# Mixer of a hybrid decoder layer: all projections as pairs of chunks with sum quads, banks swapped by halves, two heads a stage, lent ring blocks at another byte

## The chip, the cores and the metric

The kernel runs on one core of one Trainium2 chip. The metric is the device time of one execution in microseconds (us), the median of three runs. The engines are named as in the profile: PE is TensorE (matmuls; PEld loads its weights), DVE is VectorE, ACT is ScalarE, POOL is GpSimd, SP is SyncE, which issues the weight transfers.

## The reference

One layer on 256 tokens of 2048 numbers, everything in fp32: two SwiGLU blocks with the mixer between them.

```python
x = x + 0.5 * swiglu(rmsnorm(x), ffn1_w_in, ffn1_w_out)      # 2048 -> 2*5632 -> 2048
h = rmsnorm(x) @ mix_w_in                                    # 2048 -> 13312 columns
b, c, xin, p, q, k, v, gates = split(h)                      # seven of 1024, three gates of 2048
yA = (b * conv3(c * xin)) @ conv_w_out                       # causal, 3 taps
yB = (scale * group_linear(trailing_mean(p) - p)) @ pool_w_out   # windows 2, 4, 8, 16
yC = attention(q, k, v) @ attn_w_out                         # 8 heads of 128, causal, ALiBi
x = x + (sig(gA) * yA + sig(gB) * yB + sig(gC) * yC) @ mix_w_out
x = x + 0.5 * swiglu(rmsnorm(x), ffn2_w_in, ffn2_w_out)
out = rmsnorm(x)
```

## The kernel before

**Steps.** Weights stream from HBM in steps of four 128x512 blocks (`raw`, 1 MB). ACT rounds a step to its high part (`whi`, line 287), DVE subtracts that from `raw` for the low part (`wlo`, line 291), and PE does each product as three matmuls: high times high, high times low, low times high. A step is of one of three kinds. A chunk step ("C") adds into a chunk, 512 output columns for 256 tokens. A pair step ("P") adds into two chunks at once, four blocks for a quad of 256 inputs; both take 24 matmuls of 128x512. A sum step ("S", a "sum quad") computes the same quad by Strassen's and Winograd's seven products instead of eight: 21 matmuls, but DVE first builds sums of the blocks in place (lines 296 to 299, four additions of 128x512), seven blocks have to be split instead of four, and the activations of that quad need sums of their own (`sum_forms`, `sums_of_parts`). A pattern such as "SPSPSPPP" names the eight quads of a pair.

**Banks.** PSUM has eight banks of 128x512, named K1, K6, K2, K4, K7, K5, K3, K22 (0 to 7). The results of a pair end in K2 and K4 (chunk a) and K3 and K22 (chunk b). The sum products end in K1, K6, K7 and K5; DVE and ACT take them out early, behind the last S, in three pieces: `e1` (lines 529 and 530: K1, K6), `e2` (533: K7, K5) and `e3` (536: K5). At the end of the pair `results` adds them to chunk a and chunk b (542, 543).

**Side runs.** Between the halves of a step PE does small work of the mixer in the free banks (`side_psum`): eight transposes, scores of a head, products with V, the group linear. Each such function waits in a list and runs one at a time, `DELAY` and `GAP` half steps apart; its DVE and ACT work is queued right behind it, in program order.

**The mixer.** Before, the projections are 14 chunks of 4 C steps, in the order q, k (twice), v, v, then c, x, b (twice), p, p; then come gates A, B and C, each as two pairs ("SPSPSPPP", the first of A "PPPPPPPP") with two chunks of the branch's output projection behind each pair; then the output projection as four chunks. FFN1 stands ahead of the mixer and FFN2 behind it; both are pairs with sum quads already.

**Ring and units.** The split weights lie in a ring of 20 blocks. Ten of them stay; a region R of 8 and a region T of 2 are lent to the mixer as buffers ("units") between the end of FFN1 and, for R, the start of the gates, for T the start of FFN2. T's two blocks begin at bytes 185184 and 189280 of a partition; in the two FFNs 480 matmuls read them, in runs of 12.

**The first pair.** Its results are copied from their banks to `ev` (ACT line 562, DVE line 561) before the SwiGLU reads them, since the second pair wants the same banks.

Of the kernel before, what the change touches and what calls it, by code (L numbers as in the profile page):

```python
# [9 lines left out]
F32 = mybir.dt.float32  # L10
# [19 lines left out]
GATES = {(b, j): PATTERNS[0 if (b, j) == ("A", 0) else 3] for b in "ABC" for j in (0, 2)}  # L30
# [4 lines left out]
LEND = 10  # L35
REGIONS = {"R": (10, 18, "right"), "T": (18, 20, "left")}
# [35 lines left out]
def hybrid_trunk(ctx: ExitStack, tc: tile.TileContext, x, xT, wst, vecs, poolw, fnorm, consts, out):  # L72
# [118 lines left out]
    def side_psum():  # L191

        at = steps[cur[0]]
        assert side_open()
        if at["kind"] != "C":
            return wide(take(K1, K7))
        return wide(take(4, 6) if at["far"] else 6)

    def side_bank():

        at = steps[cur[0]]
        b = take(6, 7) if at["kind"] == "C" else take(K1, K6)
        return bank[:, b].rearrange("p (k s) -> p k s", s=S)
# [8 lines left out]
    def chunk(lhs, nk, evac, at=(0, 2), far=True, tail=False):  # L212


        ch = {}
        for i in range(nk):
            steps.append(dict(kind="C", lhs=lhs, i=i, first=i == 0, last=i == nk - 1, evac=evac, tail=tail,
                              chunk=ch, at=at, far=far, items=("W",)))

    def pair(forms, pattern, early, evac):  # L220
# [3 lines left out]
        mine = []  # L224
        for q, kind in enumerate(pattern):
# [13 lines left out]
            mine.append(dict(kind=kind, q=q, forms=forms, set=st, mm=mm, last=q == len(pattern) - 1, evac=evac,  # L239
# [121 lines left out]
    def emit_pair(n, half):  # L361
# [39 lines left out]
    deferred = deque()  # L401
# [76 lines left out]
    def x_side(n, j, st):  # L478
        def go():
# [47 lines left out]

    def e1():
        nc.scalar.activation(ev[:, 0], bank[:, K1], AF.Copy)
        nc.vector.tensor_sub(ev[:, 3], ev[:, 0], bank[:, K6])  # L530

    def e2():
        nc.vector.tensor_add(ev[:, 1:3], bank[:, K7:K7 + 2], ev[:, 3:4].to_broadcast((P, 2, CH)))

    def e3():
        nc.vector.tensor_add(ev[:, 3], ev[:, 1], bank[:, K5])

    def results(pattern):

        a, b = bank[:, K2:K2 + 2], bank[:, K3:K3 + 2]  # L540
# [6 lines left out]
    def in_set(n, xs, c, gs, pattern):  # L547
# [10 lines left out]
        def evac():  # L558
            a, b = results(pattern)
            if c + n == 0:  # L560
                nc.vector.tensor_copy(ev[:, 0:2], a)
                nc.scalar.activation(ev[:, 2:4], b, AF.Copy)  # L562
                a, b = ev[:, 0:2], ev[:, 2:4]
            nxt = steps[cur[0] + 1]["kind"]
            if "S" in pattern and nxt != "C":
                deferred.append((now[0] + 4, functools.partial(gate, a, b)))
# [28 lines left out]
    def ffn(n, xs, after):  # L595
# [3 lines left out]
        for p, cnt in enumerate(PARTS):  # L599
# [3 lines left out]
            for j in range(4):  # L603
# [10 lines left out]
                chunk(lambda i, c0=c0: gs[c0 + i], cnt, None if last else ev_o, at=((4, 0, 4, 2)[j],), far=False,  # L614
# [13 lines left out]
    def after1(j):  # L628
# [14 lines left out]
    xm = plain_of(x1)  # L643
# [14 lines left out]
    def ev_qk(c):  # L658
        base = keep_scaled("k", "r")

        def ev(acc):
            base(acc)
            q_, k_ = tok["q"], tok["k"]
            hold = {}

            def tr(hh):
                def go():
                    ps = side_psum()
                    for t in range(NT):
                        nc.tensor.transpose(ps[:, 0, t * P:(t + 1) * P], q_[:, t, hh * P:(hh + 1) * P], idn)  # L670
                        nc.tensor.transpose(ps[:, 1, t * P:(t + 1) * P], k_[:, t, hh * P:(hh + 1) * P], idn)
                    if hh % 2 == 0:
                        hold["qk"] = unit("qkT", F32)
                    v = hold["qk"][:, 2 * (hh % 2):2 * (hh % 2) + 2]
                    nc.scalar.activation(v, ps[:, 0:2], AF.Copy)
                    qkT[4 * c + hh] = v
                    if hh == 3:
                        drop(q_, k_)
                    if hh % 2:
                        qk_unit[4 * c + hh] = hold["qk"]  # L680
                return go
            later(*[tr(hh) for hh in range(4)])
        return ev

    def ev_v(c):
        base = keep_scaled("v")

# [10 lines left out]
    def attention(h):  # L698
# [509 lines left out]
```

## Time and profile before

| | us |
|---|---|
| median of 3 runs (lowest, highest) | 2272.11 (2270.14, 2273.11) |
| the profiled execution, its span | 2272.37, 2270.6 |
| PE, DVE, ACT busy in the span | 2250.7, 1608.9, 1084.7 |
| FFN1, projections, gates, output projection, FFN2 | 708, 368, 392, 90, 713 |

The span is what the profiler saw of the execution; 1.8 us lie around it. The stages of the last row are cut by eye at round times, where the lines of the matmuls change.

### The profile page before, as it was taken

The page shows a single profiled execution, that of the slowest core. Times are in us where ns is not written, and L with a number is a line of the kernel's source. Part 1 is how long each engine was busy: PE and PEld are TensorE (multiplying, and loading weights), DVE is VectorE, ACT ScalarE, POOL GpSimd, SP SyncE. Part 2 cuts the span into 40 slices and gives each one's busy share as a digit, 9 for nine tenths or more (in the row PEclk, how much of TensorE's full clock was granted, in tenths as well). Part 3 has the DMA queues.
Part 4 walks back from the last instruction along what each step waited for, and adds up shares of the span by engine and source line. Part 5 has one row for each costly group of instructions (what it writes and reads, how often), then busy time and mean ns, then how long its engine had stood idle before and what let it go on. Part 6 is the DMA issues. An engine that isn't in the chain of part 4 may idle for free.

```text
span 2270.6 us, 24723 instructions
## 1 busy us (share of the span) xinstructions
PE 2250.7 (99%) x10121; PEld 1857.9 (82%) x10121; DVE 1608.9 (71%) x1485; ACT 1084.7 (48%) x1040; POOL 3.7 (0%) x9
## 2 busy tenths in 40 slices
PE   9999999999999999999999999999999999999998
PEld 7888888888888888888888887888888888888887
DVE  6876885877875445555777887555876885887874
ACT  6544453454454445444555554454444453454452
POOL 0000000000000000000000000000000000000000
PEclk9999999999999999999999999999999999999999
DMA  9464564464463654455455555544564554464462
GB/s 338 167 227 147 219 222 166 173 236 167 185 241 132 220 189 182 165 203 180 185 196 212 222 201 186 209 183 178 187 230 149 221 223 149 185 241 167 186 241 93
DMA packets 65425, 442.83 MB, mean 195 GB/s; under 512 B 7328, under 2 KB 8096, under 8 KB 13472
## 3 DMA queue, kind: packets, MB, share of 16 engines
q1 hardware_dynamic: 65312, 441.26, 52.8%
q8 instruction: 79, 1.29, 0.2%
q14 instruction: 34, 0.28, 0.0%
HBM read 437.04 MB, written 4.19 MB: 194 GB/s over the span
## 4 chain that ended last, share of the span: by engine, by line
PE 87%; DVE 6%; DMA 3%; ACT 2%; issue 1%; SPq 0%; POOLq 0%; DVEq 0%; ACTq 0%
PE bank L380 44%; PE bank L368 41%; DVE wlo L291 4%; DMA raw<-w_dram 3%; PE bank L454 2%; ACT whi L287 1%; DVE raw L297 0%; DVE raw L298 0%; DVE gt L556 0%; DVE gt L555 0%; DVE raw L296 0%; DVE ev L543 0%; PE bank L838 0%; ACT junk L464 0%; DMA x0raw<-xT_dram 0%
## 5 line engine op out<-in xcount | busy, mean ns | idle before, releaser
L291 DVE TENSOR_TENSOR wlo<-raw,whi 128x2048 fp32r<-128x2048 f32 (+3 forms) x659 | 1056.7, 1640 | 474.6 <-ACT whi L287 473.4
L287 ACT ACTIVATE whi<-raw 128x2048 fp32r<-128x2048 f32 (+3 forms) x659 | 896.5, 1392 | 910.9 <-PE bank L368 297.7
L368 PE MATMUL bank<-whi,fhl 128*128 128x512 f32 x2240 | 713.2, 391 | 0.0
L368 PEld LDWEIGHTS bank<-whi,fhl 128*128 128x128 f32 x2240 | 421.1, 188 | 88.0
L368 PE MATMUL bank<-wlo,fhl 128*128 128x512 f32 x1120 | 436.6, 390 | 0.0
L380 PE MATMUL bank<-whi,gh 128*128 128x512 f32 (+1 forms) x716 | 278.1, 388 | 0.0
L380 PE MATMUL bank<-whi,gl 128*128 128x512 f32 (+1 forms) x716 | 276.7, 386 | 0.0
L380 PE MATMUL bank<-wlo,gh 128*128 128x512 f32 (+1 forms) x716 | 276.5, 386 | 0.0
L368 PEld LDWEIGHTS bank<-wlo,fhl 128*128 128x128 f32 x1120 | 210.6, 188 | 43.4
L368 PE MATMUL bank<-whi,fh 128*128 128x512 f32 x604 | 237.4, 393 | 3.6 <-ACT ev L562 2.4
L368 PE MATMUL bank<-wlo,fh 128*128 128x512 f32 x604 | 236.9, 392 | 0.5 <-DVE wlo L291 0.5
L368 PE MATMUL bank<-whi,fl 128*128 128x512 f32 x604 | 236.5, 391 | 0.0
L380 PE MATMUL bank<-whi,fhl 128*128 128x512 f32 x560 | 182.6, 393 | 0.0
L380 PEld LDWEIGHTS bank<-whi,gl 128*128 128x128 f32 x716 | 134.5, 188 | 27.6
L380 PEld LDWEIGHTS bank<-wlo,gh 128*128 128x128 f32 x716 | 134.5, 188 | 27.0
L380 PEld LDWEIGHTS bank<-whi,gh 128*128 128x128 f32 x716 | 134.5, 188 | 26.8
L368 PEld LDWEIGHTS bank<-whi,fh 128*128 128x128 f32 x604 | 114.1, 189 | 29.0 <-ACT ev L562 2.8
L368 PEld LDWEIGHTS bank<-wlo,fh 128*128 128x128 f32 x604 | 114.2, 189 | 26.1 <-DVE wlo L291 2.0
L368 PEld LDWEIGHTS bank<-whi,fl 128*128 128x128 f32 x604 | 114.1, 189 | 24.4 <-DVE fl L430 0.2
L380 PEld LDWEIGHTS bank<-whi,fhl 128*128 128x128 f32 x560 | 105.2, 188 | 21.5
L380 PE MATMUL bank<-wlo,fhl 128*128 128x512 f32 x280 | 109.0, 389 | 0.0
L607 DVE SCALAR_TENSOR_TENSOR xr<-bank,hr,xr 128x512 f32<-128x512 f32 x62 | 44.4, 750 | 69.5 <-PE bank L380 69.5
(178 smaller groups left out, 1818.4 us busy)
## 6 DMA issues: line engine op xcount, KB each, us to landing
raw<-w_dram SPq DMA_DIRECT2D x405, 1024.0 KB, 4.9
raw<-w_dram SPq DMA_DIRECT2D x8, 256.0 KB, 5.4
xr<-x_dram SPq DMA_DIRECT2D x4, 512.0 KB, 9.3
spill<-xr SPq DMA_DIRECT2D x4, 512.0 KB, 7.5
xr<-spill SPq DMA_DIRECT2D x4, 512.0 KB, 6.9
out_dram<-xr SPq DMA_DIRECT2D x8, 256.0 KB, 3.1
x0raw<-xT_dram SPq DMA_DIRECT2D x3, 512.0 KB, 7.3
raw<-w_dram SPq DMA_DIRECT2D x2, 512.0 KB, 8.1
```

Of the source, the lines that this page charges most:

```text
L287: nc.scalar.activation(hi(b, c), raw_t[n][:, i:i + c], AF.Copy)
L291: nc.vector.tensor_sub(lo(b, c), raw_t[n][:, i:i + c], f32(hi(b, c)))
L368: nc.tensor.matmul(bank[:, k], a, b, start=e["start"][at + j] and i == 0, stop=e["stop"][at + j] and i == 2)
L380: nc.tensor.matmul(acc[t], a, w[:, cols], start=g["first"] and k == 0 and i == 0, stop=g["last"] and k == KG - 1 and i == 2)
L454: nc.tensor.transpose(ps[:, i, t * P:(t + 1) * P], src(t, k), idn)
L607: nc.vector.scalar_tensor_tensor(xv, acc[:, t], half_r2(n)[:, t:t + 1], xv, op0=ALU.mult, op1=ALU.add)
```

## The change

The projections become seven pairs, p, qk0, qk1, v, cx0, cx1, b, with a pattern each; p stands first. The output projection becomes two pairs "PPPPSSPP", and the first pair of gates A gets two S. In all there are 18 more S steps and 18 fewer of the others. A pair that begins with P and follows a pair swaps the halves of PSUM (`x`, an exclusive or with 2 on the bank's number), and the copies of the very first pair go. Two heads share a stage of attention. The pool's side work is queued by time (`defer`), `side_psum` takes K1 alone in the two steps behind the last sum, only T is lent, and T's blocks begin at bytes 218080 and 222176, with a 128 byte longer tile ahead of them.

```diff
+PROJ = {"p": "PPPPPPPP", "qk0": "PPSPSPPP", "qk1": "PPSPSPPP", "v": "SPSPSPPP", "cx0": "PPPPSPPP", "cx1": "PPSPSPPP",
+        "b": "PPSPSPPP"}
+OUT = "PPPPSSPP"
+GATES = {(b, j): "PPSPSPPP" if (b, j) == ("A", 0) else PATTERNS[3] for b in "ABC" for j in (0, 2)}
-LEND = 10
-REGIONS = {"R": (10, 18, "right"), "T": (18, 20, "left")}
+LEND = 18
+REGIONS = {"T": (18, 20, "left")}
...
     def side_psum():
-        if at["kind"] != "C":
-            return wide(take(K1, K7))
-        return wide(take(4, 6) if at["far"] else 6)
+        if at["kind"] == "C":
+            return wide(6 ^ at["x"])
+        sums = at["set"]["sums"]
+        return wide((K1 if sums and sums[-1] < at["q"] < sums[-1] + 3 else take(K1, K7)) ^ at["x"])
...
     def pair(forms, pattern, early, evac):
+        x = steps[-1]["x"] if steps else 0
+        after_pair = steps and steps[-1]["kind"] != "C"
+        if after_pair and pattern[0] == "P":
+            x ^= 2
...
-                if steps and q == 0:
+                if steps and q == 0 and not after_pair:
                     mm.reverse()
...
-                nc.tensor.matmul(bank[:, k], a, b, start=e["start"][at + j] and i == 0,
+                nc.tensor.matmul(bank[:, k ^ e["x"]], a, b, start=e["start"][at + j] and i == 0,
...
         def evac():
             a, b = results(pattern)
-            if c + n == 0:
-                nc.vector.tensor_copy(ev[:, 0:2], a)
-                nc.scalar.activation(ev[:, 2:4], b, AF.Copy)
-                a, b = ev[:, 0:2], ev[:, 2:4]
...
-            rq = sp.tile([P, NT + 8], F32, tag="rq", name="rq", bufs=1)[:, :NT]
+            rq = sp.tile([P, NT + 40], F32, tag="rq", name="rq", bufs=1)[:, :NT]
...
+    def project(key, evac):
+        pair(lambda q: x1[q], PROJ[key], (e1, e2, e3), lambda: evac(*results(PROJ[key])))
...
         def scores():
             ps = side_psum()
+            for i, h in enumerate(heads):
+                qk = qkT.pop(h)
+                nc.tensor.matmul(ps[:, 2 * i, 0:P], qk[:, 0, 0:P], qk[:, 1, 0:P], start=True, stop=True,
+                                 skip_group_check=True)
+                nc.tensor.matmul(ps[:, 2 * i + 1, :], qk[:, 0, P:S], qk[:, 1, :], start=True, stop=True,
+                                 skip_group_check=True)
...
+            lazy.extend(stages[i][k] for i, k in ((0, 0), (1, 0), (0, 1), (0, 2), (2, 0), (1, 1), (1, 2), (3, 0),
+                                                  (2, 1), (2, 2), (3, 1), (3, 2)))
...
+    def pool_chain(c, p_):
+        def turn():
+            ps = side_psum()
+            transpose8(lambda t, k: p_[:, t, k * P:(k + 1) * P], ps)
+            hold["p"], hold["sum"], hold["alt"] = unit("pT", F32), unit("sum", F32), unit("alt", F32)
+            nc.scalar.activation(hold["p"], ps, AF.Copy)
+            drop(p_)
+            for i, f in enumerate((lambda: sums(0), lambda: sums(1), diff, parts)):
+                defer(2 + 2 * i, f)
...
+        later(turn, delay=DELAY + 8 * c)
+
+    project("p", ev_p)
     for c in range(2):
-        chunk(xm, 4, keep_scaled("q", "q"))
-        chunk(xm, 4, ev_qk(c))
+        project(f"qk{c}", ev_qk(c))
+    project("v", ev_v)
     for c in range(2):
-        chunk(xm, 4, ev_v(c))
-    for c in range(2):
-        chunk(xm, 4, keep_scaled("c"))
-        chunk(xm, 4, ev_u)
-        chunk(xm, 4, ev_conv(c))
-    for c in range(2):
-        chunk(xm, 4, ev_pool(c))
+        project(f"cx{c}", ev_cx(c))
+    project("b", ev_b)
...
-                            mT[j] = split_plain(ps, "m", True)
+                            for q in range(2):
+                                quad_forms(mT, 2 * j + q, ps[:, 2 * q:2 * q + 2], (1.0, 1.0), OUT[2 * j + q] == "S")
...
-    LENT = {n_ffn1 - 4: {"R": "units", "T": "units"}, n_gates: {"R": "ring"}, n_mix: {"T": "ring"}}
+    LENT = {n_gates - 2: {"T": "units"}, n_mix: {"T": "ring"}}
...
-        if n in (n_ffn1 + 10, n_ffn1 + 13, n_ffn1 + 16):
-            sums_of_parts(x1[SUMMED[(n - n_ffn1 - 10) // 3]])
-        if n == n_gates - 16:
+        if n in (n_ffn1 + 4, n_ffn1 + 7, n_ffn1 + 13):
+            sums_of_parts(x1[{4: 2, 7: 4, 13: 0}[n - n_ffn1]])
+        if n == n_ffn1 + 3:
...
-        if n == n_gates - 10:
+        if n == n_ffn1 + 8:
```

PE, in qk0, between its steps q5 and q6: the second transposition of the pool's input (`turn` of chunk 1). Line 377 is a matmul of the pair, line 468 a transpose; the bracket says which engine's semaphore the row waits for.

```order
3066 L377 MATMUL bank<-whi,fhl 128x512 x2
3067 L377 MATMUL bank<-wlo,fhl 128x512
3068 L377 MATMUL bank<-whi,fhl 128x512
3069 L468 MATMUL bank<-idn,p 128x128 [waits Activation_49]
3070 L468 MATMUL bank<-idn,p 128x128 x3
3071 L468 MATMUL bank<-idn,p 128x128 [waits DVE_49]
3072 L468 MATMUL bank<-idn,p 128x128 x3
3073 L377 MATMUL bank<-whi,fhl 128x512
```

These transposes go to banks K1 and K6, which hold sum products of qk0, so they stand behind `e1`: ACT's line 540 and DVE's line 541. Before, the projections had no sum products.

DVE at the same place, after. Lines 828 and 829 are the pool's `diff`, 505 to 508 sums of the activations' parts, 300 is `wlo`.

```order
467 L828 TENSOR_TENSOR sum<-sum,inv 128x256 x4
468 L829 TENSOR_TENSOR sum<-sum,pT 128x1024
469 L300 TENSOR_TENSOR wlo<-raw,whi 128x1024 x2
470 L505 TENSOR_TENSOR fx<-fh,fl 128x512
471 L447 TENSOR_TENSOR fx<-fx 128x128
472 L448 TENSOR_TENSOR fx<-fx 128x128
473 L449 TENSOR_TENSOR fx<-fx 128x128
474 L450 TENSOR_TENSOR fx<-fx 128x128
475 L508 TENSOR_TENSOR fl<-fx,fh 128x512
476 L300 TENSOR_TENSOR wlo<-raw,whi 128x1024 x2
477 L541 TENSOR_TENSOR ev<-ev,bank 128x512
478 L422 TENSOR_TENSOR dl<-sum,dh 128x1024
```

Ahead of these, from the end of pair p (row 442) on, DVE has 25 further rows: p's scaling, two low parts of the pool's weights, two times four additions for sum blocks, twelve `wlo` of 512 to 2048 elements, the pool's window sums. In the kernel before, the same sums of parts stand among `wlo` alone:

```order
435 L291 TENSOR_TENSOR wlo<-raw,whi 128x1024 x2
436 L498 TENSOR_TENSOR fx<-fh,fl 128x512
437 L433 TENSOR_TENSOR fx<-fx 128x128
438 L434 TENSOR_TENSOR fx<-fx 128x128
439 L435 TENSOR_TENSOR fx<-fx 128x128
440 L436 TENSOR_TENSOR fx<-fx 128x128
441 L501 TENSOR_TENSOR fl<-fx,fh 128x512
442 L291 TENSOR_TENSOR wlo<-raw,whi 128x2048 x4
```

What moved: the pool's work and that for the sums now stand in one queue with `e1`, ahead of it.

DVE, at the last chunk of the gates' branches (yC3) and the start of the output projection. First before: line 886 multiplies the chunk's accumulator with its gate, 408 is the low part of a transposed quarter of the merged branches.

```order
783 L886 TENSOR_TENSOR sg<-bank,sg 128x1024
784 L897 TENSOR_TENSOR sg<-sg 128x1024
785 L291 TENSOR_TENSOR wlo<-raw,whi 128x2048
786 L408 TENSOR_TENSOR ml<-bank,mh 128x1024
787 L291 TENSOR_TENSOR wlo<-raw,whi 128x1024 x2
788 L886 TENSOR_TENSOR sg<-bank,sg 128x1024
```

After, the same product is line 890; 447 to 461 are the chains of `sum_forms` for the two S quads of the output projection.

```order
943 L447 TENSOR_TENSOR fx<-fx 128x128
944 L448 TENSOR_TENSOR fx<-fx 128x128
945 L449 TENSOR_TENSOR fx<-fx 128x128
946 L450 TENSOR_TENSOR fx<-fx 128x128
947 L461 TENSOR_TENSOR fl<-fx,fh 128x1024
948 L447 TENSOR_TENSOR fx<-fx 128x128
949 L448 TENSOR_TENSOR fx<-fx 128x128
950 L449 TENSOR_TENSOR fx<-fx 128x128
951 L450 TENSOR_TENSOR fx<-fx 128x128
952 L461 TENSOR_TENSOR fl<-fx,fh 128x1024
953 L300 TENSOR_TENSOR wlo<-raw,whi 128x2048
954 L890 TENSOR_TENSOR sg<-bank,sg 128x1024
```

One row of 1024 became ten rows, two of which (461) wait for ACT's rounding in between; and the accumulator that line 890 reads is in banks 0 and 1, to which the second half of the output projection's first step writes.

## Rows read from the trace of the kernel before

**Rows 1.** The page, part 1: busy us, share of the span, instructions.

```profile
PE 2250.7 (99%) x10121; PEld 1857.9 (82%) x10121; DVE 1608.9 (71%) x1485; ACT 1084.7 (48%) x1040; POOL 3.7 (0%) x9
```

**Rows 2.** Stretches: length, each engine's busy us, PEclk, DMA share, GB/s.

```profile
708.00:1076.00 368.00, 368.00 (x1711) 306.26 (x1710) 192.42 (x204) 172.64 (x196) 0.70 (x1) 1.00 0.52 185
```

**Rows 3.** Timeline of TensorE, spacing: third columns on are duration, engine, line.

```profile
159.98 0.39 PE L380 MATMUL bank<-whi,gh 128*128 128x512 f32 x1
...
162.70 0.40 PE L380 MATMUL bank<-whi,gh 128*128 128x512 f32 x1
...
165.49 0.39 PE L380 MATMUL bank<-whi,gh 128*128 128x512 f32 x1
```

**Rows 4.** Timeline at the end of FFN1's first pair; wait and releaser in brackets.

```profile
51.73 0.39 PE L368 MATMUL bank<-whi,fhl 128*128 128x512 f32 x1
...
53.46 1.00 ACT L562 ACTIVATE ev<-bank 128x1024 f32<-128x1024 f32 x1
...
54.51 0.79 PE L368 MATMUL bank<-whi,fh 128*128 128x512 f32 x1 [2.40 <-ACT ev L562]
```

**Rows 5.** Timeline of TensorE in the last pair of gates C.

```profile
1415.70 0.39 PE L368 MATMUL bank<-whi,fhl 128*128 128x512 f32 x1
...
1419.94 1.11 PE L454 MATMUL bank<-idn,sg 128*128 128x128 f32 x4 [2.21 <-DVE ev L536]
1420.70 0.78 PE L368 MATMUL bank<-whi,fhl 128*128 128x512 f32 x1
```

**Rows 6.** Stretches behind these two waits; 0.50 is the granted clock.

```profile
54.40:57.70 3.30, 3.19 (x8) 2.51 (x9) 2.61 (x2) 0.66 (x2) 0.00 (x0) 0.50 0.90 328
...
1419.70:1423.00 3.30, 3.06 (x10) 2.58 (x11) 1.04 (x2) 1.91 (x2) 0.00 (x0) 0.50 0.77 271
```

**Rows 7.** Groups of VectorE by line and shape: busy us, mean ns, idle before.

```profile
L291 DVE TENSOR_TENSOR wlo<-raw,whi 128x2048 fp32r<-128x2048 f32 x269 | 613.3, 2289 | 360.5 <-ACT whi L287 359.6
L291 DVE TENSOR_TENSOR wlo<-raw,whi 128x1024 fp32r<-128x1024 f32 x180 | 215.4, 1220 | 59.2 <-ACT whi L287 59.1
L291 DVE TENSOR_TENSOR wlo<-raw,whi 128x1536 fp32r<-128x1536 f32 x95 | 166.6, 1754 | 53.1 <-ACT whi L287 53.1
L291 DVE TENSOR_TENSOR wlo<-raw,whi 128x512 fp32r<-128x512 f32 x115 | 77.9, 685 | 1.7 <-ACT whi L287 1.6
L298 DVE TENSOR_TENSOR raw<-raw 128x512 f32<-128x512 f32 x68 | 47.1, 692 | 2.3
...
L543 DVE TENSOR_TENSOR ev<-bank,ev 128x1024 f32<-128x1024 f32 x25 | 30.6, 1223 | 18.1 <-PE bank L368 18.1
...
L773 DVE SCALAR_TENSOR_TENSOR cv<-bank,vec,cv 128x255 f32<-128x255 f32 x8 | 3.8, 479 | 2.2 <-ACT cv L772 2.2
...
L713 DVE TENSOR_REDUCE sm<-e 128x1 f32<-128x256 f32 x8 | 3.4, 420 | 0.3
...
L718 DVE TENSOR_SCALAR e<-e,sm 128x256 f32<-128x256 f32 x8 | 2.8, 346 | 0.0
```

**Rows 8.** Timeline of VectorE just ahead of gates B's second pair.

```profile
1257.34 1.22 DVE L886 TENSOR_TENSOR sg<-bank,sg 128x1024 f32<-128x1024 f32 x1
...
1263.04 6.16 DVE L291 TENSOR_TENSOR wlo<-raw,whi 128x2048 fp32r<-128x2048 f32 x3 [0.45 <-ACT whi L287]
```

**Rows 9.** Timeline of TensorE at the start of that pair.

```profile
1266.96 0.39 PE L368 MATMUL bank<-whi,fh 128*128 128x512 f32 x1
1267.59 0.50 PE L368 MATMUL bank<-wlo,fh 128*128 128x512 f32 x1 [0.24 <-DVE wlo L291]
```

**Rows 10.** Timeline of TensorE around the scores of one head.

```profile
901.82 0.39 PE L380 MATMUL bank<-whi,fhl 128*128 128x512 f32 x1
...
902.93 0.39 PE L380 MATMUL bank<-wlo,fh 128*128 128x512 f32 x1
```

**Rows 11.** Timeline of TensorE around eight transposes.

```profile
1017.58 1.03 PE L454 MATMUL bank<-idn,c 128*128 128x128 f32 x8
1018.37 0.48 PE L380 MATMUL bank<-whi,fh 128*128 128x512 f32 x1
```

More of the change, by code (lines that the diff above doesn't have):

```diff
@@ L400, in hybrid_trunk, with defer @@
     lazy_at = [0]
-    deferred = deque()
+    deferred = []
+    def defer(halves, f):
+        deferred.append((now[0] + halves, f))
+        deferred.sort(key=lambda e: e[0])
     def split_plain(ps, name, keep=False):
@@ L667, in go @@
                 def go():
                     ps = side_psum()
[L669 to L675, printed above, removed]
@@ L733, in pv @@
         def pv():
-            V, pt = mx["V", h // 4], stt["pt"]
-            hs = slice(h % 4 * HD, (h % 4 + 1) * HD)
             ps = side_psum()
-            nc.tensor.matmul(ps[:, 0, :], V[:, 0, hs], pt[:, 0:S], start=True, stop=False)
-            nc.tensor.matmul(ps[:, 0, P:S], V[:, 1, hs], pt[:, S:S + P], start=False, stop=True)
-            j, k = divmod(h, 4)
+            j, k = divmod(2 * h2, 4)
+            V = mx["V", j]
+            for i in range(2):
+                pt = stt["pt", i]
+                hs = slice((k + i) * HD, (k + i + 1) * HD)
+                nc.tensor.matmul(ps[:, 2 * i, :], V[:, 0, hs], pt[:, 0:S], start=True, stop=False)
+                nc.tensor.matmul(ps[:, 2 * i, P:S], V[:, 1, hs], pt[:, S:S + P], start=False, stop=True)
@@ new lines, in ev_b, with ev_p, sums, diff @@
+            later(go, delay=DELAY + GAP * c)
+    def ev_p(a, b):
+        p1, p0 = scaled("p", b), scaled("p", a, vector=True)
+        for c, p_ in enumerate((p0, p1)):
+            pool_chain(c, p_)
+    def pool_chain(c, p_):
+        hold = {}
+        def turn():
[6 more added lines that the diff above has]
+                defer(2 + 2 * i, f)
+        def sums(gg):
+            ks = slice(2 * gg, 2 * gg + 2)
+            steps = 2 * c + gg + 1
+            src = hold["p"][:, ks]
+            for i in range(steps):
+                dst = hold["sum" if (steps - i) % 2 else "alt"][:, ks]
+                w = 1 << i
+                nc.vector.tensor_copy(dst[:, :, :w], src[:, :, :w])
+                nc.vector.tensor_add(dst[:, :, w:], src[:, :, w:], src[:, :, :S - w])
+                src = dst
+        def diff():
+            d = hold["sum"]
+            for k in range(KG):
+                nc.vector.tensor_mul(d[:, k], d[:, k], mx["inv"][:, 2 * c + k // 2])
+            nc.vector.tensor_sub(d, d, hold["p"])
+            drop(hold["p"], hold["alt"])
+            if c == 1:
+                drop(mx["inv"])
+        def parts():
+            hold["d"] = split_plain(hold["sum"], "d")
+            drop(hold["sum"])
+            later(linear)
+        def linear():
+            (wh, wl), (dh, dl) = pw[c], hold["d"]
+            ps = side_psum()
+            for gg in range(2):
+                for dd in range(2):
+                    o = ps[:, 2 * gg + dd]
+                    for cc in range(2):
+                        for i, (a, b) in enumerate(((wh, dh), (wh, dl), (wl, dh))):
+                            nc.tensor.matmul(o, a[:, gg, cc, dd * P:(dd + 1) * P], b[:, 2 * gg + cc],
+                                             start=cc + i == 0, stop=cc == 1 and i == 2, skip_group_check=True)
+            po = br_raw["B", c] = unit("po", F32, keep=True)
+            for k in range(KG):
+                nc.scalar.activation(po[:, k], ps[:, k], AF.Copy, scale=vec[:, V_PS + 4 * c + k:V_PS + 4 * c + k + 1])
+            drop(wh, wl, dh, dl)
+        later(turn, delay=DELAY + 8 * c)
@@ L1063, in hybrid_trunk @@
             if g["first"] and half == 0:
-                b = take(*g["at"]) if len(g["at"]) > 1 else g["at"][0]
-                g["chunk"]["acc"] = bank[:, b:b + 2]
+                g["chunk"]["acc"] = bank[:, g["at"]:g["at"] + 2]
             acc = g["chunk"]["acc"]
@@ L1185 @@
                 order += [a[o][0][:, (j + i) * CH:(j + i + 1) * CH] for i in range(2)]
-        order.append(a["mix_w_out"][0])
+        wo = a["mix_w_out"][0]
+        for j in (0, 2):
+            order.append(tuple(wo[:, (j + i) * CH:(j + i + 1) * CH] for i in range(2)))
     w = _stream(order)
```

281 lines of the change are left out of this document (111 added, 170 removed).

## Prediction

> **What bounds the kernel now.** I read the page first: PE is busy 99% of the span, DVE 71% [rows 1]. So time can be won only by fewer matmuls, by PE's few waits, or by a closer cadence; and it is lost wherever a wait is added. The stretches show where DVE has room: in the projections, which change most, it is busy 192 of 368 us [rows 2]. Next, the cadence: twelve matmuls of 128x512 go from 159.98 to 162.70, 0.227 us each; the twelve behind them, which read a block of T, take until 165.49, 0.2325 each [rows 3]. Last, the longest waits. At 51.73 PE stops until ACT's copy of the first pair's banks is done at 54.46 [rows 4]; in the last pair of gates C it stands from 1415.70 to 1420.70 with only two sets of four transposes between, for `e2` and `e3` [rows 5]. [...]
>
> **What is taken away.**
> - Matmuls: 18 steps lose 3 each, 54 x 0.227 = 12.2 us.
> - The wait at 51.73: 54.51 - 51.73 - 0.23 = 2.55, and eight matmuls at 0.41 instead of 0.227, 1.5 more. 4.1 us. The second pair now begins in the other halves, so nothing of it waits for the copies.
> - The wait at 1415.70: 5.00 less one matmul and 0.79 for the eight transposes [rows 11] is 4.0, and some 1.3 for the clock, 5.3. The transposes now take K1 and K6, free behind `e1` alone; some rest may stay. I take 4.6.
> - T's byte: 480 x 0.0055 = 2.6 if all its runs were as slow as that in [rows 3]; I take 2.1. The other blocks' place, modulo 256, is what T gets, so I expect their cadence. [...]
>
> Together 23.0 us. Merging heads and dropping small side runs is worth 0.3 at most: a head's scores cost PE 902.93 - 901.82 less two matmuls, 0.66 [rows 10], and as many remain.
>
> **What is added.** PE runs its queue in order, and so do DVE and ACT; a side run that needs a bank waits for the row that empties it, and that row for all ahead of it in its queue. I tested this on the kernel before. Ahead of gates B's second pair DVE has, from 1257.34, two operations of 1.22, four additions of 0.69, and two `wlo` of 2048, 2 x 2.29: 9.8 us in all, plus 0.45 of idle it shows, less an overlap of 0.09 between neighbours. So the first sum block should be ready at 1267.5; PE's next matmul begins at 1267.59, after 0.4 us too long [rows 8, 9]. (The row of three is two of 2048 and one of 1536, 6.33 by [rows 7] and 6.16 there; hence the 0.09.) DVE starts afresh at each pair's end: `results` for chunk b waits for PE, 18.1 us in 25 pairs [rows 7], and ends some 1.4 us behind it. From there I add up its rows by the durations of [rows 7] and put PE beside them (P 24 x 0.227 = 5.44, S 21 x 0.227 = 4.76, eight transposes 0.8, two heads' scores 1.3).
>
> 1. qk0, the second transposition. PE gets there 4 x 5.44 + 2 x 4.76 + 0.8 = 32.1 us after p ended. DVE until line 541: twelve of 1024 at 1.22 (14.6; nine `wlo`, two low parts, one of `diff`), two of 2048 (4.6), two of 1536 (3.5), eight raw additions (5.5), three `wlo`, two other operations and three window sums of 512, at 0.69 (5.5), four of 128x256 at 0.42 (1.7), four of 128x128 at about 0.3 (1.2), p's scaling (1.0), line 541 itself 0.7. Sum 38.3; less 1.0 for overlaps, plus some 1.5 in which DVE waits for ACT, which has its half of p and the high part of the pool's weights to do first: 39. **Wait 6.6.** This is the firmest, since nothing can be left out of it: even without idle and with all overlaps it is 4.5.
> 2. qk1, its second S: `results`, raw additions twice, the pool's last window sums (2.8), `diff` (2.9), `dl` and the `wlo` between give about 25.5 against PE's 22.0. 3.5.
> 3. v to cx0: the first scores go to banks of v's chunk b; DVE's `results` ends 1.4 behind PE. 1.5.
> 4. cx0, first products with V: behind ACT's high parts, which stand behind raw additions and the heads' maxima. 1.1.
> 5. cx1, first S: one of its banks is that of the transposes for the convolution, another that of scores. DVE: 1.4 + two of 512 (1.4) + raw 2.8 + one of 2048 (2.3) + three of 1024 (3.7) + 0.7 + eight taps of 0.48 (3.8), less 0.5, is 15.6; PE 2 x 5.44 + 0.8 + two side runs of two heads, 2.6, is 14.3. 1.2; then the softmax of two heads behind the taps, fourteen operations of up to 0.42, 4.4 in all, of which PE's other blocks cover part: 2.4 more. 3.6.
> 6. b, first S, the same taps: 1.8.
> 7. out0, second half of its first step: its bank is yC3's accumulator. From the transposes' end ACT takes about 1.9 to read them (four of 128x256, by the 0.48 of the taps), DVE's four additions 1.2, ACT's rounding 1.0 [rows 4], DVE 1.2, again 1.2 + 1.0 + 1.2, then a `wlo` of 2.3 and line 890's 1.2: 12.2. PE has one C step and a half, 8.2. 4.0.
> 8. out2's S and the linear in qk1: 2.1.
>
> Sum 24.2. Bounds: half of it if ACT and DVE overlap better than I add, one and a half times if idle within the queues is as usual as in [rows 8] (0.45 in 10). Three or four of these stop PE for more than the 2.2 after which the clock fell [rows 5, 6]; each costs about 1.4 more, so 5.6 (3 to 7.5). The additions on DVE for the 18 S steps themselves, 18 x 2.8 = 50 us, cost nothing where PE waits for no row behind them: DVE has 176 us idle in the projections.
>
> **Sum.** 2272.4 (the profiled execution, 0.26 above the median) - 23.0 + 24.2 + 5.6 = 2279.2; against the median 2279.
>
> **Rivals.**
> - *The waits don't come; faster, 2255.* Side runs and pairs change banks, and what empties them has one and a half to five steps' time. For it: in FFN1 and the gates, pairs with three S run with so few waits that PE is busy 99%. Against it: there no window sums, taps and softmax share the queue. It decides at item 1: if DVE reaches line 541 within 32 us of p's end, the rest is small too. Then only items 3 and 6 and a little of the others stay, 6 us: 2272.1 - 23.0 + 6 = 2255. [...] Chance 0.2.
> - *Half the waits: no change.* Items 1, 7 and half of the rest stay, about 17, with two clock drops, 3: 2272.1 - 23.0 + 20 = 2269. Chance 0.25.
> - *T's byte does nothing:* 2.1 on top of any case, 2281 on mine. Chance 0.2.
> - *More than I found:* each wait also delays ACT's and DVE's next rows, and idle repeats: 1.4 times the waits and five drops, 2272 - 23 + 34 + 7 = 2290. Chance 0.1.
>
> **How the numbers follow.** My forecast, items 1 to 8 about as they stand, has 0.45 and lies from 2272 to 2288; the other three that set a time have 0.2, 0.25 and 0.1. About 0.2% (4.5 us) is what can be told from no change. Faster than 2267.6: the first rival and a fifth of the second, 0.25. Slower than 2276.6: the most of the forecast and the last, 0.52. The rest, 0.23, is the same. The range takes the bounds of the waits and reaches into the first rival: 2259 to 2290; of the likeliest alone 2272 to 2288.
>
> **What would show it.** In the timeline of the changed kernel: no wait at the end of FFN1's first pair; no `e3` behind the transposes of gates C; runs of 12 at one cadence throughout; a wait of 6 to 7 us on line 541 (or ACT's 540) some 32 us into qk0 and 0.50 granted behind it; waits on line 890 in out0, 777 or 718 in cx1, 554 at cx0's start. In the stretches, the three stages of the mixer should lose as many us to waits as 18 S steps give. I am wrong if DVE at the start of each pair is further ahead than I think, above all in qk0, or if PE's 54 matmuls were not all on its path.

## The result and the profile after

The changed kernel takes 2298.21 us (median of 4 runs, 2296.60 to 2299.51) against 2272.46 of the kernel before on the same chip: a ratio of 1.0115, 95% interval 1.0097 to 1.0132. It is slower by 26 us, where the prediction had 7 and a range that ended at 2290.

The stretches, with the length, each engine's busy time, the granted clock (PEclk), DMA share and GB/s. They are cut at the first matmul of each stage: FFN1, projections, gates, output projection, FFN2.

```profile
0.00:726.70 726.70, 720.88 (x3211) 592.99 (x3212) 550.07 (x501) 359.66 (x345) 0.90 (x5) 1.00 0.55 206
726.70:1083.30 356.60, 335.31 (x1518) 276.11 (x1517) 260.33 (x320) 176.30 (x212) 0.70 (x1) 0.97 0.46 173
1083.30:1471.40 388.10, 386.21 (x1719) 318.54 (x1718) 306.17 (x289) 198.24 (x200) 0.00 (x0) 1.00 0.54 203
1471.40:1572.00 100.60, 92.56 (x397) 75.23 (x396) 76.59 (x85) 51.11 (x62) 0.00 (x0) 0.95 0.43 160
1572.00:2296.60 724.60, 713.65 (x3228) 591.24 (x3227) 539.97 (x484) 331.47 (x289) 2.10 (x3) 1.00 0.51 188
```

The reader is to see the second and the fourth row. PE is idle for 21 of 357 us in the projections and for 8 of 101 in the output projection, and there the granted clock is 0.97 and 0.95. Cut in the same way, at the first matmul of each stage as counted in both traces, the profiled executions compare thus; "over" is a stage's length less 0.2267 us for each of its matmuls, so it holds waits, slow clock and small work:

```
us            FFN1   projections (over)   gates (over)   output (over)   FFN2    span
before        730.7  327.7  (23.0)        397.2 (15.7)    90.6  (3.6)    724.4   2270.6
changed       726.7  356.6  (60.1)        388.1  (7.9)   100.7 (16.4)    724.5   2296.6
difference    -4.0   +28.9                -9.1           +10.1           +0.1    +26.0
```

The table at the head of this document cut the stages by eye, the projections from 708 to 1076 us; by their first and the gates' first matmul they go from 730.7 to 1058.4. In the kernel before, DVE is busy for 174 of these 327.7 us, so it had 153 us idle there and not 176:

```profile
730.66:1058.35 327.69, 327.69 (x1514) 272.31 (x1512) 174.26 (x184) 156.80 (x172) 0.70 (x1) 1.00 0.53 191
```

The mixer as a whole has 54 matmuls less and still takes 29.9 us longer; over its matmuls that is 42.2 us more. By the spacing of PE's rows in both traces, waits (rows that name a releaser) grew from 4.2 to 34.8 us, matmuls at the lower clock cost 11.7 us over their full speed instead of 1.2, and small work takes 32.2 instead of 30.4. The gates are shorter by 9.1, of which some 5 are small work that now runs in the projections (40 rows there instead of 80); the rest is shorter waits, a clock drop less (0.50 behind gates C's wait in [rows 6], now 1.00 from 1437 to 1443) and six matmuls less.

What PE waited for, by the line of the waiting and of the awaited instruction (total us, times, longest):

```profile
PE bank L468 <- ACT ev L540: 10.9, 7, 5.4
PE bank L377 <- DVE cv L777: 5.4, 2, 3.0
PE bank L377 <- DVE wlo L300: 5.1, 6, 1.9
PE bank L377 <- DVE sg L890: 4.5, 2, 3.9
PE bank L377 <- ACT whi L296: 3.4, 3, 1.2
PE bank L847 <- ACT qkT L681: 2.1, 1, 2.1
PE bank L377 <- DVE e L718: 1.7, 1, 1.7
PE bank L707 <- DVE ev L554: 1.3, 1, 1.3
PE bank L377 <- DVE fhl L444: 1.2, 1, 1.2
```

Of the first row's seven, six are transposes in the FFNs, 5.5 us together. The other rows name places that the prediction lists, but for some 3 us of `wlo`, `whi` and line 890 at the kernel's start, in the gates and in FFN2. The timeline of PE at the longest, the second transposition in qk0:

```profile
803.08 0.39 PE L377 MATMUL bank<-whi,fhl 128*128 128x512 f32 x1
808.90 1.12 PE L468 MATMUL bank<-idn,p 128*128 128x128 f32 x4 [5.43 <-ACT ev L540]
810.46 1.11 PE L468 MATMUL bank<-idn,p 128*128 128x128 f32 x4 [0.45 <-DVE ev L541]
811.23 0.77 PE L377 MATMUL bank<-whi,fhl 128*128 128x512 f32 x1
```

And DVE there. It starts after p's end with an idle of 3.64 for ACT's high part, works without a long break from 772.99, and ends line 541 at 810.40; p ended at 771.1, so that is 39.3 us later, where 39 was reckoned.

```profile
772.99 2.36 DVE L1019 TENSOR_TENSOR pwl<-pw,pwh 128x1024 fp32r<-128x1024 f32 x2 [3.64 <-ACT pwh L1018]
...
804.06 0.69 DVE L505 TENSOR_TENSOR fx<-fh,fl 128x512 f32<-128x512 f32 x1
...
806.50 0.69 DVE L508 TENSOR_TENSOR fl<-fx,fh 128x512 fp32r<-128x512 f32 x1 [0.69 <-ACT fh L507]
807.45 2.36 DVE L300 TENSOR_TENSOR wlo<-raw,whi 128x1024 fp32r<-128x1024 f32 x2 [0.25 <-ACT whi L296]
809.72 0.68 DVE L541 TENSOR_TENSOR ev<-ev,bank 128x512 f32<-128x512 f32 x1
```

Six times in the mixer PE worked at a granted clock of 0.50, for 3 to 6 us. Stretches of three of them:

```profile
811.20:814.20 3.00, 3.00 (x9) 2.42 (x8) 3.00 (x3) 1.02 (x1) 0.00 (x0) 0.50 0.81 322
...
998.40:1002.20 3.80, 3.80 (x10) 2.97 (x11) 2.99 (x8) 2.40 (x3) 0.00 (x0) 0.50 0.00 0
...
1478.20:1483.00 4.80, 4.80 (x12) 3.74 (x13) 2.85 (x3) 0.00 (x0) 0.00 (x0) 0.50 0.51 208
```

T's blocks in the timeline of PE: the same twelve matmuls as in [rows 3], from 162.70 to 165.49 there, now take 2.72 us, the cadence of all others.

```profile
159.20 0.39 PE L389 MATMUL bank<-whi,gh 128*128 128x512 f32 x1
...
161.92 0.39 PE L389 MATMUL bank<-whi,gh 128*128 128x512 f32 x1
```

### The profile page after: what moved, and what is told of

The parts are those of the page before. It is cut to its first block, busy times and chain, and to the rows that moved or that the text cites. A ratio compares the mean times of both kernels' runs of the same rounds, so it can differ in the third digit from the quotient of the medians.

```text
span 2296.6 us, 24928 instructions
## 1 busy us (share of the span) xinstructions
PE 2248.6 (98%) x10067; PEld 1854.1 (81%) x10067; DVE 1733.1 (75%) x1676; ACT 1116.8 (49%) x1107; POOL 3.7 (0%) x9
## 4 chain that ended last, share of the span: by engine, by line
PE 75%; DVE 15%; ACT 4%; DMA 3%; issue 2%; POOLq 0%; ACTq 0%; DVEq 0%
PE bank L377 48%; PE bank L389 25%; DVE wlo L300 9%; DMA raw<-w_dram 3%; ACT whi L296 2%; PE bank L468 1%; DVE raw L306 1%; DVE raw L307 1%; DVE raw L305 1%; DVE ev L554 1%; DVE gt L567 0%; DVE gt L566 0%; PE bank L847 0%; DVE fl L461 0%; DVE fhl L444 0%
## 5 line engine op out<-in xcount | busy, mean ns | idle before, releaser
L377 PE MATMUL bank<-whi,fhl 128*128 128x512 f32 x2992 | 956.0, 392 | 3.9 <-DVE sg L890 3.9
L377 PEld LDWEIGHTS bank<-whi,fhl 128*128 128x128 f32 x2992 | 563.8, 188 | 120.7 <-DVE sg L890 4.3
L377 PE MATMUL bank<-wlo,fhl 128*128 128x512 f32 x1496 | 583.9, 390 | 0.0
L377 PEld LDWEIGHTS bank<-wlo,fhl 128*128 128x128 f32 x1496 | 282.1, 189 | 57.2
L377 PE MATMUL bank<-whi,fh 128*128 128x512 f32 x786 | 310.7, 395 | 12.5 <-DVE cv L777 5.4
L377 PE MATMUL bank<-wlo,fh 128*128 128x512 f32 x786 | 310.0, 394 | 5.1 <-DVE wlo L300 5.1
L377 PE MATMUL bank<-whi,fl 128*128 128x512 f32 x786 | 309.6, 394 | 0.0
L377 PEld LDWEIGHTS bank<-whi,fh 128*128 128x128 f32 x786 | 149.8, 191 | 47.9 <-ACT whi L296 5.1
L554 DVE TENSOR_TENSOR ev<-bank,ev 128x1024 f32<-128x1024 f32 x34 | 41.6, 1223 | 27.6 <-PE bank L377 27.6
L306 DVE TENSOR_TENSOR raw<-raw 128x512 f32<-128x512 f32 x86 | 59.5, 692 | 3.0
L308 DVE TENSOR_TENSOR raw<-raw 128x512 f32<-128x512 f32 x86 | 59.6, 692 | 2.9
```

Of the source, the lines that this page charges most:

```text
L306: nc.vector.tensor_add(r[:, 3], r[:, 3], r[:, 2])
L308: nc.vector.tensor_add(r[:, 1], r[:, 1], r[:, 2])
L377: nc.tensor.matmul(bank[:, k ^ e["x"]], a, b, start=e["start"][at + j] and i == 0, stop=e["stop"][at + j] and i == 2)
L554: nc.vector.tensor_sub(ev[:, 2:4], b, ev[:, 2:4])
```

## The experiments

My theory: PE waits because single rows of DVE and ACT that empty a bank or finish a block stand behind long queues, and sum quads in the projections and the output projection make these queues long and occupy the banks. The main rival: pairs with side runs wait there in any case, sums or not. All edits but those that say otherwise are to the changed kernel.

**Plain patterns.** No sum quads in the projections and the output projection.

```diff
-PROJ = {"p": "PPPPPPPP", "qk0": "PPSPSPPP", ... "b": "PPSPSPPP"}
-OUT = "PPPPSSPP"
+PROJ = {"p": "PPPPPPPP", "qk0": "PPPPPPPP", ... "b": "PPPPPPPP"}
+OUT = "PPPPPPPP"
```

> The changed kernel with plain patterns: all seven projection pairs and both output pairs are PPPPPPPP (only the gates keep sum quads; the sums of activation parts are still made, unused). 16 sum steps become pair steps, 48 matmuls more, 48 x 0.227 = 10.9 us. My theory: the waits and clock drops that the changed kernel has in projections and output (about 33 and 13 us by spacing of its matmuls) come from what sum quads put into DVE's and ACT's queues and from the banks that they occupy; some 37 of them go, 2298.2 + 10.9 - 37 = 2272, and waits in the projections fall below 8 us. Rival, that pairs with merged side runs wait whether or not there are sums (side runs behind the softmax, the convolution taps and results): at least 20 us of waits stay in the projections, about 2297.

Measured: 2269.33 us, ratio to before 0.9988 (0.9978 to 0.9997). With 48 matmuls more it is 29 us faster than the changed kernel. One long wait stays in the projections, 3.8 us behind the matmul at 966.38, and it is all their waits together; the rival wanted at least 20. So it is the sum quads that bring the waits, whether by DVE's queue or by the banks isn't told by this run.

**Only the output projection plain.**

```diff
-OUT = "PPPPSSPP"
+OUT = "PPPPPPPP"
```

> The changed kernel with both output pairs PPPPPPPP: no chains of sum_forms for the merged branches, no sum blocks there; 12 matmuls more, 2.7 us. My theory: of the 9.9 us of waits and 3.4 of slow clock in the output projection 10 to 11 go (line 890 waits behind the chains, the sum step waits for its blocks): 2290.5. Rival, that the wait at the start is for the accumulator of the last chunk at whatever queue: 4 us and one clock drop stay, 2295.

Measured: 2292.39, ratio 1.0092 (1.0076 to 1.0107): 5.8 less, between the two. In the profile the stage itself did what the theory says and more: it takes 90.1 us instead of 100.7, none of its waits is left. So the rival, a wait for the accumulator at whatever queue, is out. But FFN2, in which nothing differs, took 731.9 instead of 724.5, with waits on `wlo` and on `e1` (as in FFN1, below) of 10 us instead of 3. So the stage's cost is shown; that FFN2 gives back so much here and not in the kernel of plain patterns (725.3) stays open.

**T's byte.**

```diff
-            rq = sp.tile([P, NT + 40], F32, tag="rq", name="rq", bufs=1)[:, :NT]
+            rq = sp.tile([P, NT + 8], F32, tag="rq", name="rq", bufs=1)[:, :NT]
```

> The changed kernel with the tile ahead of T 128 bytes shorter, as before the change: T's two blocks lie at 96 modulo 256 again, nothing else differs. My theory: the runs of twelve matmuls that read T take 0.2325 each instead of 0.227, in both FFNs, 2.1 us: 2300.3. [...]

Measured: 2299.65, ratio 1.0122 (1.0107 to 1.0137), 1.4 more than the changed kernel, less than what these runs can tell. The cadence tells it: the twelve matmuls above now take 2.79 us.

```profile
159.30 0.40 PE L389 MATMUL bank<-whi,gh 128*128 128x512 f32 x1
...
162.09 0.39 PE L389 MATMUL bank<-whi,gh 128*128 128x512 f32 x1
```

The byte alone changes it, so the blocks' place does matter here, 2.79 us against 2.72, 2.5% of a matmul; why, no run shows. Counted over both FFNs, the runs of twelve at this cadence are 34 in the kernel before, 35 here and none in the changed kernel; 35 x 0.07 is 2.4 us. In the profiled executions FFN1 is 0.3 longer (727.0 against 726.7) and FFN2 3.1 (727.6), but FFN2 varies by more than that between kernels that don't differ there.

**Six DVE operations moved behind line 541 in qk0.**

```diff
-        if n in (n_ffn1 + 4, n_ffn1 + 7, n_ffn1 + 13):
-            sums_of_parts(x1[{4: 2, 7: 4, 13: 0}[n - n_ffn1]])
+        if n in (n_ffn1 + 4, n_ffn1 + 7, n_ffn1 + 14):
+            sums_of_parts(x1[{4: 2, 7: 4, 14: 0}[n - n_ffn1]])
```

> The changed kernel with the sums of parts of quad 0 made one step later, so that six DVE operations stand behind line 541 in qk0 instead of ahead of it; the work itself is the same. In the changed kernel these six and their idle took from 804.06 to 807.45, 3.4 us. My theory (PE waits for DVE's queue): the wait of 5.6 us ahead of the second transposition falls to 2.2, and with it perhaps the clock drop of 1.4; 2294 to 2295, unless later rows of DVE pay it back. Rival (the wait is for the bank or for ACT's copy as such, not for the length of DVE's queue): 5.6 stays, 2298.

Measured: 2296.86, ratio 1.0112 (1.0095 to 1.0129). The wait at the second transposition fell from 6.2 us, by the spacing of its matmuls, to 3.1 (0.6 for ACT's line 540, 2.5 for line 541), as the queue's length says; and 2.2 came back at once, since the next small work, the linear, now waits for ACT's copy of the transposes. In the waits that is the last of these rows:

```profile
PE bank L468 <- DVE ev L541: 2.5, 1, 2.5
...
PE bank L847 <- ACT pT L808: 2.1, 1, 2.1
```

So the cause of this wait is settled: DVE's queue ahead of line 541. Shortening it here moved most of the gain to the next small work; the mean granted clock of the profiled execution is 0.994, where the changed kernel has 0.993.

**No side run at the start of a pair.** Small work is held back for the first half step of a projection pair.

```diff
         if not side_open():
             assert not force
             return
+        at = steps[cur[0]]
+        if not force and at["kind"] != "C" and n_ffn1 <= cur[0] < n_gates and 2 * at["q"] + now[0] % 2 < 1:
+            return
```

> The changed kernel, in which no side run starts in the first half step of a projection pair (small work that would stand there comes a half step later, and what is queued behind it too). A side run there uses banks that hold the results of the pair before. My theory (the bank is emptied 1.4 us after the pair's end): the wait of 1.5 us on line 554 at the start of cx0 goes, and that on ACT at cx1's start or before; about 2296.5, unless the later place meets a bank that is later still. Rival (the waits of heads are for ACT's and DVE's softmax, not for results): 2298, the wait is found again at the same function.

Measured: 2294.25, ratio 1.0102 (1.0086 to 1.0117), 4.0 less. The wait on line 554 at cx0's start is gone, also the next one on ACT's softmax; the stage takes 353.8 instead of 356.6. The theory holds; it had 2296.5.

**Plain patterns with a hold of two half steps.** The edit of plain patterns, and that of the hold made longer:

```diff
-        if not force and ... 2 * at["q"] + now[0] % 2 < 1:
+        if not force and ... 2 * at["q"] + now[0] % 2 < 2:
```

> The kernel of plain patterns (2269.3 us) in which no side run starts in the first two half steps of a projection pair. There the longest wait left is 3.8 us at 966.38, softmax transposes at the start of cx1 into a bank whose results line 765 still reads, and some 1.8 of slow clock behind it. Theory: both go, 5.5 us, 2264. Rival: the queue of small work is late by as much and pays it back in the gates or in waits on units, 2268 to 2269.

Measured: 2263.35, ratio 0.9960 (0.9946 to 0.9974): faster than both kernels. Theory and forecast (2264) hold. Against the kernel before, FFN1 is 4.8 us shorter and the mixer 5.4. Its stretches of the projections and of the output projection, beside those of the changed kernel above, show PE without idle time worth the name, at full clock:

```profile
725.90:1058.70 332.80, 332.40 (x1553) 277.51 (x1552) 184.90 (x231) 159.27 (x191) 0.70 (x1) 1.00 0.50 185
...
1446.30:1536.10 89.80, 89.80 (x410) 74.60 (x409) 51.12 (x56) 42.07 (x54) 0.00 (x0) 1.00 0.50 188
```

**One sum step in each pair but p.**

```diff
+PROJ = {"p": "PPPPPPPP", "qk0": "PPPPSPPP", "qk1": "PPPPSPPP", "v": "PPPPSPPP", "cx0": "PPPPSPPP", "cx1": "PPPPSPPP",
+        "b": "PPPPSPPP"}
+OUT = "PPPPPPPP"
```

> The changed kernel with one sum step in each projection pair but p (PPPPSPPP six times), none in the output pairs: against the kernel of plain patterns (2269.3 us) 18 matmuls less, 4.1 us. Theory (each wait is the length of DVE's queue ahead of one row): in qk0 DVE's queue is shorter by one set of four additions and three split blocks, 39 - 4.6 = 34.4 us against 32.8 of TensorE, a wait of 1.6; at cx0's start 1.5; two linears some 2 each; none at the sum step itself in cx1 and b, since it stands at the fifth quad: 2269.3 - 4.1 + 6.5 = 2271.7. Rival (it is the presence of sum products in the banks, not the queue's length): a wait of 3 to 6 and a clock drop in each pair as in the changed kernel, at least 2282.

Measured: 2272.62, ratio 1.0002 (0.9993 to 1.0011). The rival is out, and the total is as forecast, but by luck in its parts: the wait in qk0 is 5.0 us, not 1.6, and the others are smaller. The mean granted clock of the profiled execution is 0.998, with plain patterns 0.999. DVE had less to do ahead of its row and was hardly earlier, since it stood idle for ACT's high part, which waited until PE had freed blocks of the ring:

```profile
788.06 1.92 ACT L295 ACTIVATE whi<-raw 128x2048 fp32r<-128x2048 f32 x1 [5.49 <-PE bank L376]
790.01 2.29 DVE L299 TENSOR_TENSOR wlo<-raw,whi 128x2048 fp32r<-128x2048 f32 x1 [4.69 <-ACT whi L295]
```

So the length of the queue alone doesn't give a wait; how far DVE can run ahead counts too.

**FFN1's first pair as before.** Copies, and no swap of halves for the second pair.

```diff
-        if after_pair and pattern[0] == "P":
+        if after_pair and pattern[0] == "P" and len(steps) != 8:
...
-                if steps and q == 0 and not after_pair:
+                if steps and q == 0 and (not after_pair or len(steps) == 8):
...
             a, b = results(pattern)
+            if c + n == 0:
+                nc.vector.tensor_copy(ev[:, 0:2], a)
+                nc.scalar.activation(ev[:, 2:4], b, AF.Copy)
+                a, b = ev[:, 0:2], ev[:, 2:4]
```

> The changed kernel with the first pair of FFN1 as before the change: its results are copied out by DVE and ACT, and the second pair uses the same halves of PSUM. Theory: the wait of 2.5 us at its end and 1.5 of slow clock come back, 2302.2. Rival (what is won there is given back in FFN1, where ACT's first piece of the sum products waits behind a weight transfer): the later waits of FFN1 shrink by as much, 2299 to 2300.

Measured: 2298.96, ratio 1.0119 (1.0104 to 1.0134), 0.75 more. The medians can't tell the two forecasts apart, the trace can. The wait is back, 2.0 us behind the matmul at 51.85 (the granted clock is 1.00 over the first 100 us, where the kernel before has 0.98), but FFN1 ends at 727.3, only 0.6 later: the transposes' waits for `e1` in FFN1 fell from 4.0 to 2.1 us. The rival is right. The chain of FFN1 shows what these waits hang on. First before, then the changed kernel (start, us, what):

```profile
316.15 6.67 DMA raw<-w_dram
...
322.90 2.01 ACT whi L287 x2
324.91 0.49 ACT ev L529
```

```profile
312.26 6.67 DMA raw<-w_dram
...
319.01 2.10 ACT whi L296 x3
321.12 0.49 ACT ev L540
```

In both a transfer that takes 6.67 us is on the path; ACT's first piece of the sum products stands behind the high part that waits for it, and the transposes behind that piece. In the changed kernel and in the eleven others here with three raw buffers FFN1 ends between 725.7 and 727.3; of these eleven, this run and that of T's byte are the two that differ within FFN1.

**One chain of sums for the output pairs.**

```diff
-OUT = "PPPPSSPP"
+OUT = "PPPPSPPP"
```

> The changed kernel with PPPPSPPP instead of PPPPSSPP in the two output pairs: of the two chains of sum_forms behind each turn of the merged branches one goes, 6 matmuls more, 1.4 us. Theory (the chains and their handovers between ACT and DVE make the waits there): the chain of 3.4 us is replaced by some 1.9 of plain forms, so the wait of 4.0 on line 890 falls to about 2.5; of the 4.8 us at 1546 to 1552 in the second pair the part at the second sum step, 3.4, goes; one of two clock drops (1.7) too: 2298.2 + 1.4 - 1.5 - 3.4 - 1.7 = 2293. Rival (one sum step is enough to keep the waits, as both blocks and banks of it are as late): 2298 to 2299.

Measured: 2293.33, ratio 1.0095 (1.0080 to 1.0110). The total is as forecast, its parts only by half. The wait on line 890 fell from 4.0 us to 1.8, as the theory has it; but the second pair's sum step kept its 3.3 (1.2 for `whi`, 2.0 for `wlo`), as the rival has it, and what went there is the 1.4 that PE waited for a bank. The mean granted clock is 0.991 to 0.994 in its four runs and 0.991 to 0.993 in those of the changed kernel, which doesn't tell whether one drop went.

**The sum step of cx1 and b two quads later.**

```diff
-PROJ = {... "cx1": "PPSPSPPP", "b": "PPSPSPPP"}
+PROJ = {... "cx1": "PPPPSPPP", "b": "PPPPSPPP"}
```

> The changed kernel with PPPPSPPP instead of PPSPSPPP in cx1 and b: the sum step at the third quad, whose banks are those of the convolution's transposes and of scores, becomes a pair step; 6 matmuls more, 1.4 us. Theory (place of the sum step right behind the taps): waits of 2.5, 2.0 and 3.2 at 992, 996 and 1047 go, and two clock drops, 3.4: 2298.2 + 1.4 - 11 = 2288.6. Rival (DVE's load in these pairs is what waits, wherever the sum step stands): the wait comes back at the fifth quad's blocks or at line 541, at most 4 us gained, 2294 or more.

Measured: 2291.95, ratio 1.0081 (1.0064 to 1.0098), 6.3 less, between both. The waits of 2.5, 2.0 and 3.2 on the taps and the scores are all gone, so the sum step's place made them; a wait of 2.2 for line 552 (553 in the changed kernel) came at cx1's start. The mean granted clock of the profiled execution is 0.993, as in the changed kernel. The three stages of the mixer take 9.6 us less, and FFN2 6 us more.

**A fourth raw buffer** (edit to plain patterns with the hold).

```diff
-RAW_BUFS = 3
-RING = 20
-LEND = 18
-REGIONS = {"T": (18, 20, "left")}
+RAW_BUFS = 4
+RING = 18
+LEND = 16
+REGIONS = {"T": (16, 18, "left")}
```

> The kernel of plain patterns with the hold (2263.4 us), a fourth buffer for raw weights, and 18 instead of 20 blocks in the ring to make room. In the FFNs of all kernels here ACT's first piece of the sum products waits behind a high part whose weights have just landed, and FFN1 ends between 725.7 and 727.3 whether or not 2 to 4 us are saved within it. Theory (the weights' stream is the floor: a transfer starts only when DVE frees a raw buffer): with a fourth buffer these waits, about 1.5 each in six or seven places, go, and FFN1 ends near 722: 2263.4 - 8 = 2255. Rival (HBM itself, or the ring's smaller size): the same waits, or new ones on free ring blocks, 2263 or more.

Measured: 2268.66, ratio 0.9985 (0.9976 to 0.9994), 5.3 slower than with three. With three buffers ACT's waits have the row below (total us, times, longest); with four that wait is 12.3 us in 11 times. Transposes wait for `e1` only once by more than 0.3 us; instead steps wait for `wlo`, about 1 us in each of eight places, and FFN1 ends at 730.0. So the transfers did hold `e1` up, but this form of the cure, with the smaller ring, costs more.

```profile
ACT whi L295 <- DMA raw<-w_dram: 158.4, 82, 4.3
```

**Three sum steps** (edit to plain patterns with the hold): PPPPSPPP in v, cx1 and b.

> The kernel of plain patterns with the hold (2263.4 us) and one sum step (PPPPSPPP) in v, cx1 and b, where the kernel with one sum in each pair showed the smallest waits: 9 matmuls less, 2.0 us; one wait of about 1 on line 541 and smaller ones come with it: 2262.7. Rival: the sums bring a clock drop again, 2265 or more.

Measured: 2264.09, ratio 0.9963 (0.9948 to 0.9977): the same as without them, between the two forecasts; the mean granted clock is 0.999 in each of its runs, against 0.998 to 0.999 without them. 2 us of matmuls go for 1 us of waits and what FFN1, gates and FFN2 vary by.

## Why the prediction was wrong

The sign and the mechanism were right, the size was not: it forecast 7 us and 26 came. Two terms of the sum were put too small, item 8 (2.1, measured 7.0) and the clock (5.6, measured 11.7); what is taken away came to 20.2 of 23.0, and 4 us were in no item. By its own steps:

- *Waits 1 to 7* stand where they were placed. Measured from the spacing of the matmuls, with the forecast behind: qk0 6.2 (6.6), qk1's sum step 3.4 (3.5), cx0's start 1.5 (1.5), products with V 0.8 (1.1), cx1 4.5 (3.6), b 3.2 (1.8), out0 4.0 (4.0): 23.6 together, where 22.1 were forecast. Edits of their own show the cause for qk0, cx0's start, cx1, b and out0; for qk1 and the products with V it is argued from the rows. For qk0 the close sum of 39 is in part luck. DVE's rows there take 35.2 us, not 37.3, since p's scaling was done before p ended and the rest is 1.1 shorter; its idle is 4.1, not 1.5.
- *The step that failed first: item 8.* It was put down without a reckoning: out2's sum steps and the linear at 2.1, and they measured 4.8 and 2.2. In out2, DVE's queue holds the chains that make FFN2's activations, ahead of the sum blocks, and DVE stands idle in each of them for ACT, which I had not added. This is the same mistake as in cx1 and b, where the taps wait twice for ACT's scaling. PE's three waits in out2, the first for a bank that these chains read, the others for blocks:

```profile
1547.71 0.50 PE L377 MATMUL bank<-whi,fh 128*128 128x512 f32 x1 [1.24 <-DVE fhl L444]
...
1552.49 0.51 PE L377 MATMUL bank<-whi,fh 128*128 128x512 f32 x1 [1.04 <-ACT whi L296]
1554.89 0.50 PE L377 MATMUL bank<-wlo,fh 128*128 128x512 f32 x1 [1.89 <-DVE wlo L300]
```

The timeline of DVE in out2 and in b:

```profile
1533.46 1.23 DVE L461 TENSOR_TENSOR fl<-fx,fh 128x1024 fp32r<-128x1024 f32 x1 [1.19 <-ACT fh L460]
1534.60 0.48 DVE L444 SCALAR_TENSOR_TENSOR fhl<-bank,vec,fhl 128x256 fp32r<-128x256 f32 x1
1535.62 0.48 DVE L444 SCALAR_TENSOR_TENSOR fhl<-bank,vec,fhl 128x256 fp32r<-128x256 f32 x1 [0.54 <-ACT fhl L443]
```

```profile
1046.68 0.48 DVE L775 SCALAR_TENSOR_TENSOR cv<-bank,vec,cv 128x255 f32<-128x255 f32 x1 [0.54 <-ACT cv L774]
...
1049.13 0.48 DVE L775 SCALAR_TENSOR_TENSOR cv<-bank,vec,cv 128x255 f32<-128x255 f32 x1 [0.54 <-ACT cv L774]
```

- *The clock: the second step that failed.* 5.6 us for four drops was too little. There were six, of 1.6 to 2.6 us each, 11.7 together; both the count and the price of about 1.4 were low. I had counted waits above 2.2. In qk1 two waits of 1.12 and 1.85, one matmul apart, were followed by a granted clock of 0.51, while one of 2.1 at 868 and one of 1.83 in FFN2 were followed by 1.00. Nor does the length of the waits tell: those of 2.3 and 1.7 in cx1 were followed by 0.50, the same two, 2.3 and 1.8, in the run with six operations moved by 1.00 (the row below). What decides is open.

```profile
995.10:998.00 2.90, 2.90 (x13) 2.40 (x14) 2.16 (x6) 2.55 (x5) 0.00 (x0) 1.00 0.00 0
```

- *What is taken away.* The 54 matmuls are all gone, 12.2. The wait in gates C fell: that pair has 2.5 us over its matmuls instead of 6.6, 4.1 against 4.6 forecast. T's cadence is 0.2267, as forecast. But the wait at FFN1's first pair and T's byte together brought 4.0 in FFN1 and nothing in FFN2, 3.9 of 6.2. The prediction didn't look for what takes the rest: the transposes' waits for `e1` grew from 1.9 to 4.0 us in FFN1 and from 2.0 to 2.5 in FFN2. The experiment on the first pair shows that they take back what is saved ahead of them, that with a fourth buffer that they hang on the weights' transfers; for FFN2 it is argued.
- *The remaining 4 us or so* are smaller waits that weren't listed, on lines 541 in v and cx1 (0.8 and 0.6) and at the start of gates A and B (0.4 and 0.5), and 2 us of small work, which was put at 0.3 less than before.
- *The range.* It was to take the bounds of the waits, half to one and a half times 24.2, and of the drops, 3 to 7.5. By these the sum is 2264 to 2293, so 2290 was too low by its own terms; 2298 lies outside both.

The rivals: that the waits don't come, or half of them, fell with the first profile. T's byte has its effect on the cadence, 2.79 us for twelve matmuls against 2.72; in the time of the whole kernel no run here shows it. "More than I found", 2290, came nearest and had 0.1.

## What to carry to other kernels

Adding up the rows ahead of one instruction on its engine, and putting the other engine's time beside it, found seven of eight items within about 1.4 us before any run; to find the size as well, add the idle that each handover between two engines leaves in such a queue (0.5 to 1.2 us a time here), and carry the sum through every pair, not the plainest ones. Fewer matmuls were worth nothing where the engine that prepares them was late for PE: 48 of them put back, and side work kept away from the banks of the last results, made 2263.35 of 2298.21. A gain ahead of a stage that waits for a stream of transfers can be given back there, as 1.4 of 2.0 us were in FFN1; measure it at the end of that stage.

## What the runs showed of the hardware

Twelve matmuls that read a block of T took 2.79 us in the kernel before and in the run of T's byte, and 2.72 in the changed kernel, where T lies 128 bytes further on than in that run. A transfer of 1 MB whose median to landing is 4.9 us takes 6.5 to 6.8 at the places that lie on the path of FFN1 (6.78, 6.67, 6.46, 6.51 in the changed kernel's chain, which picks out the late ones).
